# A hybrid decoder block: 576 dense tokens instead of 640, dot products of one gathered tile in the front, and the low parts of v on POOL

## The chip, the cores and the metric

The kernel runs on one core of a Trainium2 chip. The metric is the time of one execution on the device in microseconds; lower is better. The core has a matrix engine (PE), a vector engine (DVE), an activation engine (ACT) and POOL, which also issues the indirect loads; SP issues most other loads and stores. All of them work side by side, each through its own queue, in order.

## The reference

One decoder layer over 1,024 tokens of width 1,024: a mixing part (gated convolution and sliding-window attention) and then a retrieval of experts (PEER). The second part is what the change is about. With `h` the normalised and modulated rows, for each token:

```python
q = (ht @ wq).reshape(t, PEER_HEADS, 2, PEER_DK)          # 8 heads, two halves
sa = einsum('thd,hnd->thn', q[:, :, 0], keys[0]); sb = ...  # 128 scores each
va, ia = top_k(sa, 16); vb, ib = top_k(sb, 16)
cand = va[..., :, None] + vb[..., None, :]                # 256 pairs
top, pos = top_k(cand, 16)
eidx = 128 * ia + ib at pos                               # 16 of 16384 experts for each head
g = softmax(top)
u = u_tab[eidx]; v = v_tab[eidx]                          # 128 rows of 1024 for each token
a = gelu(einsum('thkd,td->thk', u, ht))
out = einsum('thk,thkd->td', g * a, v)
x = x + g2 * out
```

All of it is float32. The kernel computes large products as three products of rounded parts (high times high, high times low, low times high), so each operand is split into a high part (a cast, made by ACT) and a low part (the difference, made by DVE or POOL).

## The kernel before, in words

The expert part is computed in two ways at once. For the *dense* tokens all 16,384 experts are multiplied: the gate weights of a token are spread over a table of 128 x 128 (`spread`, L655), `up` (L779) multiplies all rows of u with the tokens, `weigh1` and `weigh2` apply gelu and the table and split the result, and `down` (L835) multiplies with all rows of v and adds into `dacc`. For the *gathered* tokens, in tiles of 128, `gather` (L691) fetches for each of the 128 chosen experts one row of u for each token (one indirect load of 128 rows, 0.524 MB, issued by POOL at L713), takes its dot product with h on DVE (L732), and then fetches the rows of v and adds them up with their weights on DVE (L740). Before, tokens 0 to 639 are dense and 640 to 1,023 gathered (three tiles).

The front (L307) runs over groups of 384, 384 and 256 tokens: projections (`proj`, L235; 42 for each group, whose low parts POOL makes at L244), attention, the output projection, the rows of x2 and h2 for later, and the scores and choice of keys. While the second and third group pass through the front, the tokens of the group before are chosen and spread: `finish_topk` (L540) with `select` (L565) and `spread`. In a step of `spread` four tokens get their indicator rows `oi` (by ACT, POOL or DVE, as the pattern HOT says, L672 to L679), one DVE instruction makes `oj` (L683) and PE multiplies them.

The dense stage (L750) begins when the front is done. Its loop (L956) goes over j = 4 to 128; a period g is four values of j. In each j `usplit` loads the rows of u for j + 1 and splits them (high on ACT at L771, low on POOL at L772), `up(j)` issues 48 matmuls (L788); in two of four j there is a `down` (L845). The rows of v are loaded and split by `vload` (L820), high on ACT (L831), low on DVE (L832), through a staging tile `vraw` with two buffers: rows 0 to 3 for the first half of the columns before or with phase 0 and 1, rows 0 to 2 for the second half one after another in the first steps of the first `down`, row 3 after it.

What sets the order: `bg(us)` (L202) gives each background task a credit, and a task runs one step for each whole credit; the gather has a rate of 0.49 for each us of credit in the dense stage (L943), the spreading 0.94 in the front. `usplit` gives 2 x 3.2 us, each of the ten steps of `down` in a period 2.57, a projection 24 T / 2400 + 0.5. The dense loop stands in `manual_schedule` (L955), and the trace has POOL's instructions there in the order in which the code is written; in front the order is a planner's. The gather holds a ring of six rows, five in flight.

Of the kernel before, what the change touches and what calls it, by code (L numbers as in the profile page):

```python
# [10 lines left out]
F32 = mybir.dt.float32  # L11
# [10 lines left out]
P = 128  # L22
# [23 lines left out]
DT0, DT = 0, 640  # L46
G0 = 640
GT = 3
J = 4
TB = 32  # L50
HOT = "APVV"
RATE0, RATE = 0.0, 0.49
# [10 lines left out]
TM = 384  # L63
RING = 6
XB = 4
# [9 lines left out]
def hymba_peer_kernel(ctx: ExitStack, tc: tile.TileContext, a, out: bass.AP):  # L75
# [5 lines left out]
    gat = ctx.enter_context(tc.tile_pool(name="gat", bufs=1))  # L81

# [27 lines left out]
    x2d = dram.tile([S, D], F32, name="x2d")  # L110
    h2d = dram.tile([GT * P, D], F32, name="h2d")
# [38 lines left out]
    def ada(parts, ap, ring, sums=None):  # L150
        n = 0
        for i in parts:
            acc = sums if sums is not None and i == parts[0] else ap.tile([P, D], F32, name="acc", bufs=1)
# [9 lines left out]
            if i < 5:  # L163
                mps = pm.tile([P, 8], F32, name="pm")
                for m in range(NC):
                    PE.matmul(mps[:, m:m + 1], acc[:, P * m:P * (m + 1)], ones[:, 0:1], start=True, stop=True)
                V.tensor_add(mod[:, 8 * i:8 * i + 8], mps, cols[:, COLS["b"][0] + 8 * i:COLS["b"][0] + 8 * i + 8])
            else:
                b2 = ap.tile([P, D], F32, name="b2", bufs=1)
# [12 lines left out]
    def bias_table(ap):  # L182
# [6 lines left out]
        rb = ap.tile([32, NH, P], F32, name="rb", tag="acc", bufs=1)  # L189
# [61 lines left out]
    def norm_stats(chunk, T):  # L251
        pt = pj.tile([P, TM], F32, name="pj")
        for c in range(NC):
            sq = tmp("sq")
            A.activation(sq[:, 0:T], chunk(c), AF.Square)
            PE.matmul(pt[:, 0:T], onesd, sq[:, 0:T], start=(c == 0), stop=(c == NC - 1))
        r = tmp("rstd", bufs=2)
# [32 lines left out]
    def group_stats(chunks, T):  # L290
        pt = pj.tile([P, TM], F32, name="pj")
        for i, src in enumerate(chunks):
            sq = tmp("sq")[:, 0:T]
# [13 lines left out]
    def front(t0, T, hs, nxt):  # L307
        nb = T // P
        nd = max(0, min(nb, (DT - t0) // P))
# [68 lines left out]
        halves = gat.tile([P, 2, 4, 2 * P], F32, name="halves", tag="more")  # L378
# [100 lines left out]
        def to_rows(dst, r0, b, srcs, idn):  # L479
            for h in range(2):  # L480
# [10 lines left out]
                nc.sync.dma_start(dst[r0 + P * b:r0 + P * b + P, 512 * h:512 * h + 512], xt)  # L491

        for b in range(nb):
            to_rows(x2d, t0, b, [x2T], ident)
        if ROWS:
            modulate2()
        for b in range(nb):
            if b >= nd:
                to_rows(h2d, t0 - G0, b, [h2H, h2L], identr)
        if nd:  # L500
            for k in range(2):
                for c in range(NC):
                    src = ch(h2[k], c)[:, 0:P * nd].bitcast(F32)
                    at = slice(t0 - DT0, t0 - DT0 + P * nd)
                    nc.sync.dma_start(h2s[k, :, c, at], src)
# [6 lines left out]
        va = [lv.tile([P, 2 * PH, 16], F32, name="va", bufs=5) for b in range(nb)]  # L512
        iu = [lv.tile([P, 2 * PH, 16], U32, name="iu", bufs=5) for b in range(nb)]
        def keys(ms, qs):
            sc = []
            for b in range(nb):
# [3 lines left out]
                s = lv.tile([P, 2, P], F32, name="sc", bufs=4)  # L520
# [19 lines left out]
        def finish_topk():  # L540
            for b in (range(nb) if ORDER else [*range(nd, nb), *range(nd)]):
                r = yield from select(va[b], iu[b])
                if b < nd:
                    yield from spread(t0 // P + b, *r)
                else:
                    place((t0 - G0) // P + b, *r)
                    placed.append(b)
                    if len(placed) == 1:
                        gtask.append(add(gather(), RATE0))
# [15 lines left out]
    def select(va, iu):  # L565
# [63 lines left out]
        for s, src in ((0, aab), (1, stb)):  # L629
            r = ft(f"pick{s}", tag=("a3", "st3")[s])  # L630
            hot1 = sel.tile([P, PH, 16, 16], BF16, name="hot1")
            V.tensor_tensor(hot1, src.rearrange("p (h k) -> p h k", h=PH).unsqueeze(2).to_broadcast([P, PH, 16, 16]),
# [470 lines left out]
```

## Time and profile before

| | us |
|---|---|
| median of 3 runs | 2,877.46 |
| lowest and highest run | 2,875.39 and 2,883.49 |
| span of the profiled execution | 2,871.6 |

The profile is one execution, whose span was 2,871.6 us. An engine's busy time is the time in which it ran at least one instruction; matmuls overlap in a pipeline, so the duration of one is longer than the distance from one to the next. A group of instructions is those of one line, engine and shape; the idle time beside it is that of the engine just before them, with what ended it. The chain of waits goes back from the last instruction to whatever released each step.

### The profile page before, as it was taken

Reading aid. Unit: us, or ns where it says so; the run is one execution under the profiler, and the core shown is the slowest. Engines: PE = TensorE matmul, PEld = TensorE weight load, DVE = VectorE, ACT = ScalarE, POOL = GpSimd, SP = SyncE. Lnnn points to the kernel's source line nnn. Section 1 sums busy time; section 2 is a strip of 40 time slices with the busy share of each in tenths; the row PEclk is TensorE's granted clock in tenths of the full one; section 3 lists DMA queues with packets and bytes.
Section 4 is the critical chain, followed back from the end, with each engine's and each line's share of the span. In section 5 each row is a group of like instructions: output and inputs, shape, how many; then the busy total and the mean of one; then the engine's idle time right before and its main releaser. Section 6 shows DMA issues by size and latency. Waiting matters only on the chain.

```text
span 2871.6 us, 44952 instructions
## 1 busy us (share of the span) xinstructions
PE 2710.1 (94%) x15567; PEld 2441.8 (85%) x15567; DVE 2391.0 (83%) x4853; ACT 1095.5 (38%) x2193; POOL 1727.9 (60%) x1491
## 2 busy tenths in 40 slices
PE   5999989899888889999999999999999999999998
PEld 3888978788687779889999898999999889989997
DVE  5665899878799778888888898888988888888886
ACT  2455467775476633322222232222223222222221
POOL 3534476665676745666666666666666666656661
PEclk7999989999899989999999999999999999999999
DMA  6647423355334576999999999999999999999995
GB/s 224 230 145 232 123 85 129 139 199 181 99 145 138 203 234 202 347 333 348 331 320 346 348 348 333 348 323 334 337 349 323 324 349 333 331 331 342 331 334 185
DMA packets 345032, 763.69 MB, mean 266 GB/s; under 512 B 31418, under 2 KB 130138, under 8 KB 341860
## 3 DMA queue, kind: packets, MB, share of 16 engines
q0 software_dynamic: 112320, 408.99, 39.2%
q1 hardware_dynamic: 231044, 349.21, 36.4%
q8 instruction: 122, 2.00, 0.3%
q10 hardware_dynamic: 1440, 2.62, 0.2%
q14 instruction: 106, 0.87, 0.1%
HBM read 701.45 MB, written 59.24 MB: 265 GB/s over the span
## 4 chain that ended last, share of the span: by engine, by line
PE 44%; DMA 8%; DVE 6%; issue 4%; POOL 2%; ACT 1%; SPq 0%; DVEq 0%; POOLq 0%; ACTq 0%
PE pv L845 23%; PE pa L788 21%; DMA vraw<-in_v 4%; DMA uraw<-in_uT 2%; DVE pq L740 1%; DVE vdL L832 1%; DVE rows L732 1%; DMA wraw<-in_wq 1%; DVE wdL L815 1%; DVE dacc L864 1%; ACT vdH L831 1%; POOL rows L713 1%; DVE more L732 1%; POOL uL L772 0%; DVE gw L807 0%
## 5 line engine op out<-in xcount | busy, mean ns | idle before, releaser
L788 PE MATMUL pa<-h,uH 128*128 128x320 f32 x4096 | 772.0, 310 | 14.5 <-ACT uH L771 6.3
L788 PEld LDWEIGHTS pa<-h,uH 128*128 128x128 f32 x4096 | 648.2, 189 | 22.0 <-ACT uH L771 7.3
L244 POOL TENSOR_TENSOR wL<-wraw,wH 128x512 fp32r<-128x512 f32 x252 | 360.7, 1440 | 263.2 <-ACT wH L243 224.8
L845 PE MATMUL pv<-vdH,wdH 128*128 128x512 f32 x1275 | 500.2, 392 | 14.7 <-DVE dacc L864 14.5
L845 PE MATMUL pv<-vdL,wdH 128*128 128x512 f32 x1275 | 498.1, 391 | 0.1
L845 PE MATMUL pv<-vdH,wdL 128*128 128x512 f32 x1275 | 497.1, 390 | 0.0
L788 PE MATMUL pa<-h,uL 128*128 128x320 f32 x2048 | 468.9, 310 | 2.9 <-POOL uL L772 2.9
L772 POOL TENSOR_TENSOR uL<-uraw,uH 128x512 fp32r<-128x512 f32 x256 | 343.6, 1343 | 149.5 <-ACT uH L771 140.3
L713 POOL DMA_INDIRECT rows<-in_u,eidx x257 | 259.1, 1008 | 164.7 <-DVE aw L732 100.0
L713 POOL DMA_INDIRECT rows<-in_v,eidx x254 | 252.5, 994 | 160.9 <-DVE pq L740 115.6
L788 PEld LDWEIGHTS pa<-h,uL 128*128 128x128 f32 x2048 | 344.0, 189 | 3.8 <-POOL uL L772 3.8
L740 DVE SCALAR_TENSOR_TENSOR pq<-rows,aw,pq 128x1024 f32<-128x1024 f32 x253 | 324.7, 1284 | 5.0 <-DMA rows<-in_v,eidx 2.5
L864 DVE TENSOR_TENSOR dacc<-dacc,pv 128x512 f32<-128x512 f32 x310 | 212.2, 685 | 137.5 <-PE pv L845 136.7
L831 ACT CAST vdH<-vraw 128x512 fp32r<-128x512 f32 x255 | 152.7, 619 | 437.1 <-DMA vraw<-in_v 386.2
L732 DVE CUSTOM_DVE_ANT_0 rows<-rows,pq 128x1024 f32<-128x1024 f32 x257 | 307.8, 1214 | 10.5 <-DMA rows<-in_u,eidx 10.1
L771 ACT CAST uH<-uraw 128x512 fp32r<-128x512 f32 x256 | 158.4, 620 | 384.1 <-DMA uraw<-in_uT 374.1
L845 PEld LDWEIGHTS pv<-vdH,wdH 128*128 128x128 f32 x1275 | 240.0, 188 | 70.9 <-DVE dacc L864 23.1
L845 PEld LDWEIGHTS pv<-vdH,wdL 128*128 128x128 f32 x1275 | 240.0, 188 | 50.6
L845 PEld LDWEIGHTS pv<-vdL,wdH 128*128 128x128 f32 x1275 | 240.1, 188 | 47.6 <-DVE vdL L832 0.5
L678 POOL TENSOR_SCALAR oi<-iota,tr 128x128 f32<-128x128 f32 x160 | 198.5, 1242 | 109.8 <-PE gps L686 89.4
L832 DVE TENSOR_TENSOR vdL<-vraw,vdH 128x512 fp32r<-128x512 f32 x255 | 193.7, 776 | 74.1 <-ACT vdH L831 73.6
L814 ACT CAST wdH<-gw 128x640 fp32r<-128x640 f32 x128 | 93.1, 728 | 402.6 <-DVE gw L807 393.7
(251 smaller groups left out, 5118.7 us busy)
## 6 DMA issues: line engine op xcount, KB each, us to landing
uraw<-in_uT SPq DMA_DIRECT2D x256, 256.0 KB, 6.3
vraw<-in_v SPq DMA_DIRECT2D x255, 256.0 KB, 6.0
gd<-stage SPq DMA_DIRECT2D x20, 2048.0 KB, 7.5
gt<-gd SPq DMA_DIRECT2D x160, 256.0 KB, 10.2
wraw<-in_w_in SPq DMA_DIRECT2D x108, 256.0 KB, 2.8
wraw<-in_wq SPq DMA_DIRECT2D x96, 256.0 KB, 2.8
wt<-in_w_ada SPq DMA_DIRECT2D x40, 512.0 KB, 4.7
wraw<-in_w_out SPq DMA_DIRECT2D x48, 256.0 KB, 2.7
```

What stands on the lines that cost most here:

```text
L244: G.tensor_tensor(wL, w, wH.bitcast(F32), op=ALU.subtract)
L678: (G if who == "P" else V).tensor_scalar(oi, iota, tr[:, 0, t:t + 1], tr[:, 2, t:t + 1], op0=ALU.is_equal, op1=ALU.mult)
L713: G.indirect_dma_start(out=r, out_offset=None, in_=table, in_offset=bass.IndirectOffsetOnAxis(ap=eidx[:, ti, k:k + 1], axis=0))
L732: V.tensor_tensor_reduce(out=r, in0=r, in1=h2, op0=ALU.mult, op1=ALU.add, scale=1.0, scalar=0.0, accum_out=aw[:, k:k + 1])
L740: V.scalar_tensor_tensor(acc, r, aw[:, k:k + 1], acc, op0=ALU.mult, op1=ALU.add)
L771: A.copy(uH, raw)
L772: G.tensor_tensor(uL, raw, uH.bitcast(F32), op=ALU.subtract)
L788: PE.matmul(AT[j][:, s, 0:n], l[:, c, :], h2[r][4 * h + c][:, s * n:s * n + n], start=(h == 0 and c == 0 and k == 0), stop=(h == 1 and c = ...
L831: A.copy(vH, raw)
L832: V.tensor_tensor(vL, raw, vH.bitcast(F32), op=ALU.subtract)
L845: PE.matmul(pt, l[:, P * tt:P * tt + P], r, start=(m == 0), stop=(m == 3 * J - 1))
L864: V.tensor_tensor(dst, dst, pt, op=ALU.add)
```

## The change

- **Tokens.** Dense are tokens 128 to 703 (576), gathered are 0 to 127 and 704 to 1,023 (448), in four tiles of 128, 64, 128 and 128. The tile of 64 puts half of each token's experts on the other 64 partitions, has 64 fetches of u and of v, and its two halves are added by a second, accumulating store.
- **Early dot products.** A ring of four rows (`rowring`) lives through the kernel. From the second group on a task runs the first 129 units of the gather (h and all 128 dot products of tile 0) on three of its rows, with h in the fourth, at a rate of 0.5; what is left of it is drained before the dense stage. In the dense stage the gather goes on with eight rows, seven in flight.
- **Dense products.** `up` runs over two halves of 288 columns, one PSUM bank each (three buffers). `down` takes the rows of v as the stationary operand and 288 tokens as the moving one: 16 outputs of 12 matmuls for a period, where there were 10 of 12 with 512 columns. The sum is kept transposed, and the last step multiplies with g2 and adds x2 in one instruction. A second output holds the dense tokens transposed, and the host only puts rows in place.
- **Low parts of v** are made by POOL instead of DVE.
- **Small.** u is loaded in one DMA for each j (two buffers of that); the pattern of the indicator rows gives DVE three of eight instead of four; the choice of keys works on four heads at a time; some staging buffers are fewer.

The diff, cut to its core:

```diff
-DT0, DT = 0, 640
-G0 = 640
-GT = 3
+DT0, DT = 128, 576
+HN = DT // 2
+GTILES = [(0, 128), (704, 64), (768, 128), (896, 128)]
-HOT = "APVV"
-RATE0, RATE = 0.0, 0.49
+HOT = "APVAVAPV"
+RATEA, RATE = 0.5, 0.5
+GPLAN = []
+for _gi, (_, _w) in enumerate(GTILES):
+    GPLAN += [("h", _gi, 0)] + [("u", _gi, k) for k in range(_w)]
+    GPLAN += [("v", _gi, k) for k in range(_w)] + [("g", _gi, 0), ("x", _gi, 0)]
+NA = 129
-XB = 4
+XB = 3
+    rowring = gat.tile([P, 4, D], F32, name="ring")
...
-        for b in range(nb):
-            to_rows(x2d, t0, b, [x2T], ident)
+        for b, gi in gblocks.items():
+            g0, w = GTILES[gi]
+            to_rows(x2d, GOFF[gi], P - w, b, [x2T], ident)
...
+            for h0 in range(0, PH, 4):
+                hs = slice(h0, h0 + 4)
+                hot1 = sel.tile([P, 4, 16, 16], BF16, name="hot1")
...
+    def gather(plan, slots, held=None):
...
+        ring, at = [], 0
+        for kind, gi, k in plan:
+            while gi not in placed:
                 yield
+            while at < len(plan) and len(ring) < len(slots) - 1 and plan[at][1] in placed:
+                ring.append(fetch(plan[at]))
+                at += 1
             r = ring.pop(0)
+            w = GTILES[gi][1]
+            if kind == "h":
+                h2 = held if held is not None else env["pq"].tile([P, D], F32, name="pq")
+                A.copy(h2, r)
+                aws[gi] = gat.tile([P, P], F32, name="aw", bufs=2)
+            elif kind == "u":
                 V.tensor_tensor_reduce(out=r, in0=r, in1=h2, op0=ALU.mult, op1=ALU.add, scale=1.0,
-                                       scalar=0.0, accum_out=aw[:, k:k + 1])
+                                       scalar=0.0, accum_out=aws[gi][:, k:k + 1])
...
+                if w < P:
+                    A.copy(r[0:w, :], acc[0:w, :])
+                    G.dma_start(at_out, r[0:w, :], accum_op=ALU.add)
...
-                    raw = da.tile([P, 4, P], F32, name="uraw", bufs=2)
-                    nc.sync.dma_start(raw, a["uT"][j, :, 4 * h:4 * h + 4, :])
+                    if h == 0:
+                        both = da.tile([P, NC, P], F32, name="uraw", bufs=2)
+                        nc.sync.dma_start(both, a["uT"][j])
+                    raw = both[:, 4 * h:4 * h + 4, :]
...
             A.copy(vH, raw)
-            V.tensor_tensor(vL, raw, vH.bitcast(F32), op=ALU.subtract)
+            G.tensor_tensor(vL, raw, vH.bitcast(F32), op=ALU.subtract)
...
-            for tt in range(nt):
-                bg(2.57)
-                next(extra, None)
-                pt = pv.tile([P, 512], F32, name="pv")
...
+            for x in range(4):
+                for s in range(2):
+                    bg(1.6)
+                    next(extra, None)
+                    pt = pv.tile([P, 512], F32, name="pv")
+                    m = 0
+                    for j in js:
+                        vH, vL = VV[j, dh]
+                        for l, r in ((vH, W[j][0]), (vH, W[j][1]), (vL, W[j][0])):
+                            PE.matmul(pt[:, 0:n], l[:, P * x:P * x + P], r[:, s * n:s * n + n],
+                                      start=(m == 0), stop=(m == 3 * J - 1))
...
-            if g == P // J - 1:
-                V.tensor_tensor(dst, dst, fin["g2"][dh], op=ALU.mult)
-                V.tensor_tensor(dst, dst, fin["x2"][tt, dh], op=ALU.add)
-                A.dma_start(out[r0:r0 + P, ds], dst)
+            if g == last:
+                V.scalar_tensor_tensor(dst, dst, mod[:, 40 + dc:41 + dc], fin[dc][:, s * n:s * n + n],
+                                       op0=ALU.mult, op1=ALU.add)
+                A.dma_start(outT[:, dc, s * n:s * n + n], dst)
...
-        pv = es.enter_context(tc.tile_pool(name="pv", bufs=2, space=PSUM))
+        pv = es.enter_context(tc.tile_pool(name="pv", bufs=3, space=PSUM))
...
+        if not gtask:
+            gtask.append(add(gather(GPLAN[:NA], [rowring[:, x, :] for x in range(3)], rowring[:, 3, :]), RATEA))
         hs, ft = front(t0, T, hs, nxt)
         drain(prev)
         prev = ft
+    drain(gtask[0])
```

## Rows read from the trace of the kernel before

**Rows 1.** The page's first part: busy time, share of the span, instructions.

```profile
PE 2710.1 (94%) x15567; PEld 2441.8 (85%) x15567; DVE 2391.0 (83%) x4853; ACT 1095.5 (38%) x2193; POOL 1727.9 (60%) x1491
```

**Rows 2.** Stretches: length, busy of engines (instructions), PE clock, DMA share, GB/s.

```profile
345.00:740.00 395.00, 358.81 (x2220) 323.98 (x2220) 336.82 (x1126) 261.64 (x616) 245.63 (x190) 0.97 0.41 143
740.00:1050.00 310.00, 261.70 (x1826) 232.49 (x1824) 254.38 (x904) 195.03 (x459) 211.05 (x161) 0.92 0.44 155
...
903.00:953.00 50.00, 40.89 (x300) 37.44 (x299) 47.76 (x94) 29.76 (x69) 41.86 (x30) 0.97 0.48 168
...
1176.00:2810.00 1634.00, 1623.92 (x9117) 1479.29 (x9118) 1426.94 (x1851) 436.79 (x708) 1049.34 (x974) 1.00 0.96 337
```

**Rows 3.** Chain of waits, one dense period: start, length, engine, tile, line, count.

```profile
1356.36 13.62 PE pv L845 x60
1369.98 21.11 PE pa L788 x144
1391.10 13.62 PE pv L845 x60
1404.72 7.04 PE pa L788 x48
```

**Rows 4.** Groups of POOL, 1,300 to 2,500 us: busy us, mean ns, idle before.

```profile
L772 POOL TENSOR_TENSOR uL<-uraw,uH 128x512 fp32r<-128x512 f32 x172 | 230.6, 1340 | 82.1 <-ACT uH L771 75.2 <-PE pa L788 4.6
L713 POOL DMA_INDIRECT rows<-in_u,eidx x187 | 186.7, 998 | 116.0 <-DVE aw L732 73.6 <-issue 18.4 <-DMA out<-rows 12.7
...
L713 POOL DMA_INDIRECT more<-in_v,eidx x87 | 89.0, 1023 | 44.7 <-DVE pq L740 32.4 <-issue 9.1 <-DMA uraw<-in_uT 0.7
```

**Rows 5.** Timeline of PE in the third front: start us, us, instruction.

```profile
1023.07 0.28 PE L247 MATMUL pj<-h2L,wH 128*128 128x256 f32 x1
...
1025.20 0.28 PE L247 MATMUL pj<-h2L,wH 128*128 128x256 f32 x1
```

**Rows 6.** Timeline of POOL in the dense stage: start us, us, instruction, [idle before].

```profile
1719.52 0.95 POOL L713 DMA_INDIRECT rows<-in_u,eidx  x1
1720.78 0.94 POOL L713 DMA_INDIRECT rows<-in_u,eidx  x1 [0.30 <-DVE gw L807]
1721.74 1.31 POOL L772 TENSOR_TENSOR uL<-uraw,uH 128x512 fp32r<-128x512 f32 x1
1723.20 1.36 POOL L713 DMA_INDIRECT more<-in_u,eidx  x1 [0.16 <-issue]
```

**Rows 7.** DMA issues, 1,300 to 2,500 us: count, KB each, us to landing.

```profile
vraw<-in_v SPq DMA_DIRECT2D x171, 256.0 KB, 6.2
```

**Rows 8.** A group of ACT, 1,300 to 2,500 us, columns as in rows 4.

```profile
L831 ACT CAST vdH<-vraw 128x512 fp32r<-128x512 f32 x170 | 101.5, 619 | 290.1 <-DMA vraw<-in_v 252.8 <-PE pv L845 36.8
```

**Rows 9.** Waits, 1,300 to 2,500 us: who for whom, us, times, longest.

```profile
DVE vdL L832 <- ACT vdH L831: 37.5, 29, 3.2
```

**Rows 10.** Groups of DVE, 1,300 to 2,500 us, columns as in rows 4.

```profile
L732 DVE CUSTOM_DVE_ANT_0 rows<-rows,pq 128x1024 f32<-128x1024 f32 x188 | 225.5, 1214 | 10.3 <-DMA rows<-in_u,eidx 9.9
L740 DVE SCALAR_TENSOR_TENSOR pq<-rows,aw,pq 128x1024 f32<-128x1024 f32 x168 | 215.6, 1284 | 1.7
L864 DVE TENSOR_TENSOR dacc<-dacc,pv 128x512 f32<-128x512 f32 x215 | 147.3, 685 | 98.1 <-PE pv L845 97.7
L832 DVE TENSOR_TENSOR vdL<-vraw,vdH 128x512 fp32r<-128x512 f32 x170 | 128.8, 775 | 37.6 <-ACT vdH L831 37.5
```

**Rows 11.** Groups of DVE, 345 to 1,050 us; last row before that.

```profile
L678 DVE TENSOR_SCALAR oi<-iota,tr 128x128 f32<-128x128 f32 x320 | 129.7, 443 | 24.4 <-PE gps L686 22.4
L683 DVE TENSOR_TENSOR oj<-iota,tr 128x512 f32<-128x512 f32 x160 | 118.9, 764 | 8.2 <-PE gps L686 4.2 <-ACT tr L662 3.2
...
L161 DVE SCALAR_TENSOR_TENSOR acc<-wt,cond,acc 128x1024 f32<-128x1024 f32 x31 | 47.5, 1532 | 6.7 <-DMA wt<-in_w_ada 6.4
```

**Rows 12.** A stretch of 20 us, columns as in rows 2.

```profile
2640.00:2660.00 20.00, 20.00 (x105) 17.64 (x104) 17.32 (x18) 2.56 (x4) 12.24 (x13) 1.00 1.04 390
```

More of the change, by code (lines that the diff above doesn't have):

```diff
@@ L152, in ada @@
         for i in parts:
-            acc = sums if sums is not None and i == parts[0] else ap.tile([P, D], F32, name="acc", bufs=1)
+            acc = sums if sums is not None and i == parts[0] else rowring[:, 0, :]
             for c in range(NC):
@@ L376, in front @@
         mc, ma = bigt(bb, "mc", F32R), bigt(bb, "ma", F32R)
[L378 removed]
+        halves = t1.tile([P, 2, 4, 2 * P], F32, name="halves")
         def attention():
@@ L540, in finish_topk @@
         def finish_topk():
-            for b in (range(nb) if ORDER else [*range(nd, nb), *range(nd)]):
+            for s0, b in blocks:
                 r = yield from select(va[b], iu[b])
[L543 to L549, printed above, removed]
+                lo, hi = max(s0, DT0), min(s0 + P, DT0 + DT)
+                if hi > lo:
+                    yield from spread(s0, lo - s0, hi - s0, *r)
+                if b in gblocks:
+                    place(gblocks[b], *r)
+                    placed.append(gblocks[b])
         return hn, finish_topk()
@@ L688, in spread, with rows_of, fetch @@
                 yield
-            nc.sync.dma_start(gd[(ti * P - DT0) // TB + q], stage)
-    def gather():
+            nc.sync.dma_start(gd[(s0 - DT0) // TB + q], stage)
+    def gather(plan, slots, held=None):
         state = {"n": 0}
-        rows = gat.tile([P, 4, D], F32, name="rows", tag="stage"), gat.tile([P, RING - 4, D], F32, name="more")
         def row():
-            n = state["n"] % RING
+            n = state["n"] % len(slots)
             state["n"] += 1
-            return rows[n // 4][:, n % 4, :]
-        def fetch(u):
-            ti, n = divmod(u, 2 * P + 2)
+            return slots[n]
+        def rows_of(r, src, gi, whole=True):
+            w = GTILES[gi][1]
+            part = src[GOFF[gi]:GOFF[gi] + w, :]
+            G.dma_start(r[P - w:P, :], part)
+            if w < P and whole:
+                G.dma_start(r[0:w, :], part)
+        def fetch(unit):
+            kind, gi, k = unit
@@ L715, in fetch @@
-            return r
-        total = GT * (2 * P + 2)
-        ring = [fetch(u) for u in range(RING - 1)]
-        for u in range(total):
-            while (u + RING - 1) // (2 * P + 2) >= len(placed) and len(placed) < GT:
+            elif kind == "x":
+                rows_of(r, x2d, gi, whole=False)
+            else:
+                G.indirect_dma_start(out=r, out_offset=None, in_=a[kind],
+                                     in_offset=bass.IndirectOffsetOnAxis(ap=eidx[:, gi, k:k + 1], axis=0))
@@ L940, in ahead @@
                 weigh2(j)
-        for t in gtask:
-            t[1], t[2] = RATE, GC0
+        rows = gat.tile([P, 4, D], F32, name="rows", tag="stage")
+        slots = [rows[:, x, :] for x in range(4)] + [rowring[:, x, :] for x in range(4)]
+        add(gather(GPLAN[NA:], slots), RATE, GC0)
         m = 0
```

241 lines of the change are left out of this document (114 added, 127 removed).

## The prediction, made before the run

> **What bounds the kernel now.** I read the busy shares first: PE 94%, DVE 83%, POOL 60% [rows 1]. The windows by stage then show two kernels in one. In the two front stages (345 to 740 and 740 to 1,050 us) DVE is the fullest beside PE, 336.8 of 395 and 254.4 of 310 us, and neither is full. In the dense stage (1,176 to 2,810) PE is busy for 1,623.9 of 1,634 us, beside DMA at a share of 0.96 and 337 GB/s [rows 2]. The chain of waits in the dense stage is PE alone for long stretches: 60 matmuls of L845 in 13.62 us, 144 of L788 in 21.11, 60 in 13.62, 48 in 7.04, together 55.4 us [rows 3]. That is one period, four values of j. The measured period is 55.8 us: L772 makes the low part of u twice for each j, and its 172 instructions stand in 1,200 us, so 13.95 us for each j [rows 4]. So PE is the pace, with 0.4 us lost in each period. The question is what PE costs afterwards, and which engine is next.
>
> **PE.** From the chain a 320-column matmul takes 21.11/144 = 0.1466 us and a 512-column one 0.227 [rows 3]; a 256-column one of the front takes (1025.20 - 1023.07)/18 = 0.118 [rows 5]. Between 256 and 320 columns lie 288, at 0.1325 us. The columns shrink by a tenth, the fixed part of each matmul stays, and the down product issues 192 matmuls of 288 columns in a period where it issued 120 of 512; up has 192 as before. So PE needs 384 x 0.1325 = 50.9 us, 4.5 less than 55.4.
>
> **POOL in the dense stage.** The credits for the gather give (4 x 6.4 + 16 x 1.6) x 0.5 = 25.6 fetches in a period (before: (25.6 + 25.7) x 0.49 = 25.1). POOL makes 8 low parts in a period today, all of u; the 8 of v come to it, so 16. A low part takes 1.34 us in the mean, a fetch 1.00 to 1.02 [rows 4]. The timeline shows what busy time hides: from one fetch to the next 1.26 us pass (1719.52 to 1720.78) though the fetch itself takes 0.95; a low part behind a fetch starts at once, and a fetch behind a low part 0.15 us after it [rows 6]. In the written order the 16 low parts stand in 11 runs, so 11 gaps of 0.15 and 14.6 of 0.30 make 6.0 us. Best case, with the short durations of the timeline: 25.6 x 0.94 + 16 x 1.31 + 6.0 = 51.0 us. With the means: 25.6 x 1.00 + 16 x 1.34 + 6.0 = 53.0. I take the middle, 51.9, as DVE gives up 8 instructions that read the same memory beside it. POOL alone then needs more than PE.
>
> To that comes a wait. The staging tile of v has two buffers. In the second half of a period's v, the third row set can be loaded only when the low part of the first is made. Its load lands 6.2 us after issue [rows 7], and ACT casts it in 0.62 [rows 8]: 6.8 us. Between the two, POOL has one more low part and 1.6 fetches with their gaps, about 3.3 us, as the down steps now come every 12 matmuls of 288 columns. It stands still for the other 3.5. Today the same wait stands on DVE, whose steps are longer: 37.5 us in 21.5 periods, 1.7 each [rows 9]. Behind a standing POOL are queued the next fetches and low parts; DVE is covered by seven rows in flight, PE by the low parts made one j ahead, and both only put off the wait, since POOL never catches up. So the period is 51.9 + 3.5 = 55.4 us. Bounds: 51.3 (no wait; PE's 50.9 with today's loss) and 56.5 (means, the whole wait). Against 55.8 that is -0.4 us in 1,634/55.8 = 29.3 periods: **-12 us**.
>
> **DVE and DMA in the dense stage** are not next. DVE is busy for 87% of 55.8 us, 48.7, today [rows 2]; 8 x 0.775 of v go, and 16 adds of 288 columns at about 0.45 stand for 10 of 0.685 [rows 10] (between 0.385, in proportion, and the 0.685 of the whole; 0.45 as part of it is fixed): 43 of 55.4. A period moves 25.6 fetches of 0.524 MB, 2.1 MB each of u and v, and 18 instead of 20 blocks of the gate table: 18.8 MB, at 55.4 us 339 GB/s, today's rate. Faster, it would become a bound (rival 2).
>
> **Front.** The 128 dot products of tile 0 are new here, as tokens 0 to 127 leave the dense part. Their task starts with the second group and earns 0.5 for each us of credit: 42 projections x 4.34 x 0.5, less what passes until tile 0 is chosen, some 86 units in that group, the rest in the third. The fetches are POOL's, about 1 us each; it is idle for 248 of these 705 us [rows 2]. On DVE a unit costs at least the 1.20 us of busy time that L732 shows with its second operand in PSUM [rows 10]. Here both operands lie in SBUF, and the nearest row with two of 1,024 columns, the accumulation of L161, has 1,532 ns [rows 11] against 1,284 for L740, whose sum is in PSUM [rows 10]. Bounds 1.20 and 1.61 (1.53 and a twentieth for the read of the sum), value 1.40 between them: 179 us. Taken away: half a block of spreading, and an eighth of the indicator rows, which pass from DVE to ACT. Today 160 steps cost 129.7 + 118.9 = 248.6 us [rows 11]; 144 steps of 1.5 x 0.405 + 0.743 = 1.35 us cost 195, so -54. Picking in halves of four heads doubles 12 instructions of a block, in six blocks here, each with a fixed part between nothing and the 0.44 us of a whole small one (L678), 0.15 taken: +11. Together +136 on 591 us of DVE in 705. The fullest stretch of the rows has DVE at 47.8 of 50 us, 95.5% [rows 2]; at that share 727 us need 761: **+56 us**. Bounds: 702 us of work at 100% give -3, 754 at 95.5% +84.
>
> The Trainium skill ("SBUF — State Buffer", section "Who interferes with whom") has a rule against exactly these units: a VectorE instruction with two SBUF inputs and a GpSimd instruction that reads SBUF lock each other out for the whole instruction. The slow L161 agrees with it. By the rule alone the units would go at the upper bound, and the whole would come to 2,940.
>
> **Small terms.** Nine up products before the steady part: 432 x 14.1 ns, -6 us. The last two down products and one closing instruction instead of three: -3. Fewer, larger stores of h2 and four blocks of x2 turned to rows instead of eight lie under the front's DVE; without that cover they give a few us. The second write of the 64-token tile waits on POOL for its first, once, about one landing (6.2). The smaller counts of staging buffers in front get nothing, as no row prices them.
>
> **Sum.** 2,871.6 (span) + 56 - 12 - 6 - 3 = 2,906.6. The median of the three runs, 2,877.46, lies 5.9 us above this span, so I forecast 2,912; its own range is 2,875 to 2,965. A difference below 0.3% (8.6 us) counts as no change.
>
> **Rivals.**
> 1. PE stays the pace (the faster side). Its place is POOL's queue at the third v load: if POOL runs behind and finds its tiles ready, the wait is gone, and with fetches at 0.94 POOL needs 51.0. The point is a POOL period below 51.3 us. Price: -4.5 x 29.3 = -132, with +56 - 9: span 2,786.6, **2,792**. For it: POOL is idle for 36% of the dense stage today, mostly for DVE's rows, and eight row slots instead of six ease that. Against: the 51.0 is a floor without one wait.
> 2. DMA becomes the pace. 337 GB/s at 0.96 is 351 at a full share: 18.8 MB in 53.6 us, -64 + 47: **2,860**. For it: 0.96 over 1,634 us. Against: one stretch of 20 us has 390 GB/s [rows 12], so a full share is no wall.
> The skill ("DMA: Bandwidth & Descriptors", section "Bandwidth") gives some 358 GB/s as a core's part of HBM; that would be 52.5 us and 2,828, but the 390 lies above it.
> 3. The front swallows the dot products: DVE's 114 idle us take them, as PE has a block less to spread in the second group. +5 instead of +56: **2,861**.
> 4. Both prices at their upper ends, period 56.5 and front +84: +21 instead of -12, and +28: **2,973**. Early units that are late (two rows in flight) and drained before the dense part belong here too.
>
> **Chances.** Forecast 0.46, rival 1 0.20, rival 2 0.11, rival 3 0.12, rival 4 0.11. Faster by over 0.3% is rival 1, most of 2, half of 3 and a little of the forecast: 0.37. Within 0.3%: 0.11. Slower: 0.52. The range 2,790 to 2,985 leaves out half of rival 1 and less than half of rival 4.
>
> **What would show it.** Right: POOL busy for 90% or more of the steady part, with little idle time before fetches and a wait for ACT's cast before the low parts of v; PE's matmuls 0.1325 us apart with gaps before L845's successor put down to POOL; a period near 55.4 us; DVE above 90% from 345 us on, and the dense part beginning some 50 us later. If PE runs through at 51 us a period, or the front is no longer than before, the forecast is wrong.

## Result, and the profile after

The kernel became slower: 3,149.03 us against 2,876.7, a ratio of 1.0943 (95% interval 1.0915 to 1.0971). The forecast was 2,912 with a range up to 2,985, so the time lies outside it. The profiled execution after has a span of 3,152.8 us, 281.2 more than before.

The first matmul of the up product ends the front. It starts at 1,045.5 us before and at 1,266.7 after: front +221.2 us, where the forecast had +56. What follows took 1,826.1 us and takes 1,886.1: +60.0, where the forecast had -21. Both terms failed, the front by more.

The page's first part (answers to [rows 1]): PE is busy for about as long as before (2,710.1 us) in a longer span, POOL for 428 us more, DVE for only 44 more.

```profile
PE 2707.2 (86%) x17743; PEld 2548.0 (81%) x17743; DVE 2435.5 (77%) x5083; ACT 1115.6 (35%) x2420; POOL 2155.8 (68%) x1865
```

The windows of the two front stages and of the dense stage, columns as in [rows 2]. DVE is busy for 422.82 of 507 and 321.68 of 402 us, 82%, not the 95.5% that the forecast took; PE's granted clock is 0.83 and 0.85. In the dense stage PE is busy for 1,189 of 1,300 us.

```profile
357.00:864.00 507.00, 383.85 (x1964) 330.18 (x1964) 422.82 (x1244) 244.95 (x580) 328.50 (x257) 0.83 0.60 199
864.00:1266.00 402.00, 309.62 (x1917) 273.38 (x1915) 321.68 (x983) 241.68 (x582) 249.61 (x205) 0.85 0.50 170
1500.00:2800.00 1300.00, 1189.05 (x8628) 1171.86 (x8627) 1010.36 (x1519) 330.47 (x640) 1035.66 (x943) 0.97 0.93 327
```

Groups of the front after (357 to 1,266 us; columns as in [rows 4]). The early products (L759) take 179.1 us, 1,407 ns each: the term of the forecast to the microsecond. Beside them stand the early fetches on POOL, 1,260 ns each instead of "about 1 us", with 121.6 us of standing still before them.

```profile
L759 DVE CUSTOM_DVE_ANT_0 ring<-ring 128x1024 f32<-128x1024 f32 x128 | 179.1, 1407 | 36.4 <-DMA ring<-in_u,eidx 36.4
L707 DVE TENSOR_TENSOR oj<-iota,tr 128x512 f32<-128x512 f32 x144 | 105.0, 733 | 19.0 <-PE gps L710 17.6 <-ACT tr L686 0.6
L702 DVE TENSOR_SCALAR oi<-iota,tr 128x128 f32<-128x128 f32 x216 | 102.0, 475 | 66.3 <-PE gps L710 64.2 <-PE pm L408 1.0 <-PE pj L257 0.4
...
L254 POOL TENSOR_TENSOR wL<-wraw,wH 128x512 fp32r<-128x512 f32 x164 | 231.5, 1421 | 71.2 <-ACT wH L253 59.3 <-PE pj L257 4.5 <-PE pm L533 4.5
L741 POOL DMA_INDIRECT ring<-in_u,eidx x128 | 161.2, 1260 | 121.6 <-DVE aw L759 48.7 <-DVE oi L702 24.9 <-issue 9.9
L702 POOL TENSOR_SCALAR oi<-iota,tr 128x128 f32<-128x128 f32 x144 | 159.1, 1105 | 119.0 <-PE gps L710 104.7 <-ACT oi L699 9.3 <-ACT tr L686 2.3
```

The waits of PE in the same stretch (who for whom: us, times, longest): for POOL's indicator rows, for DVE's, for POOL's low parts of the weights. Each is short, and each holds the projections queued behind it on PE.

```profile
PE gps L710 <- POOL oi L702: 34.2, 36, 3.6
PE gps L710 <- DVE oi L702: 29.8, 25, 4.9
PE pj L257 <- POOL wL L254: 25.7, 32, 2.2
```

POOL's groups in the dense stage after (1,500 to 2,800 us; columns as in [rows 4]):

```profile
L862 POOL TENSOR_TENSOR vdL<-vraw,vdH 128x512 fp32r<-128x512 f32 x183 | 244.0, 1346 | 62.1 <-ACT vdH L861 58.6 <-issue 1.7
L803 POOL TENSOR_TENSOR uL<-uraw,uH 128x512 fp32r<-128x512 f32 x180 | 233.1, 1295 | 2.7 <-ACT uH L802 0.6
L741 POOL DMA_INDIRECT ring<-in_u,eidx x160 | 156.7, 979 | 51.1 <-issue 28.6 <-DVE aw L759 11.0 <-DMA out<-ring 6.2
L741 POOL DMA_INDIRECT rows<-in_u,eidx x160 | 156.7, 979 | 56.8 <-issue 27.5 <-DVE aw L759 20.4 <-DMA out<-rows 2.2
L741 POOL DMA_INDIRECT ring<-in_v,eidx x123 | 121.6, 989 | 39.1 <-issue 23.2 <-DVE pq L768 9.3 <-DVE dacc L895 4.5
L741 POOL DMA_INDIRECT rows<-in_v,eidx x123 | 119.8, 974 | 42.0 <-issue 20.7 <-DVE pq L768 12.5 <-DVE dacc L895 4.9
```

And the waits of the same stretch that matter. PE stands still for a bank of the up product that DVE's gw has to free; POOL for ACT's cast; the two rows of "issue" are the gaps around POOL's own fetches.

```profile
PE pa L817 <- DVE gw L836: 85.1, 38, 8.4
POOL vdL L862 <- ACT vdH L861: 58.6, 36, 3.3
POOL ring L741 <- issue: 51.8, 210, 0.6
POOL rows L741 <- issue: 48.2, 187, 0.6
```

The 180 low parts of u between the 60th and the 240th make 22.5 periods. Their starts give 58.02 us a period after and 56.42 before. These periods make 35.9 of the 60.0 us. Another 25.2 lie between the first matmul of the up product and the 60th low part (421.0 us after, 395.8 before; 385.1 in e2, which has no low parts of v); the rest of the stage is 1.1 us shorter.

### The profile page after: what moved, and what is told of

The parts are those of the page before. It is cut to its first block, busy times and chain, and to the rows that moved or that the text cites. A ratio compares the mean times of both kernels' runs of the same rounds, so it can differ in the third digit from the quotient of the medians.

```text
span 3152.8 us, 49815 instructions
## 1 busy us (share of the span) xinstructions
PE 2707.2 (86%) x17743; PEld 2548.0 (81%) x17743; DVE 2435.5 (77%) x5083; ACT 1115.6 (35%) x2420; POOL 2155.8 (68%) x1865
## 4 chain that ended last, share of the span: by engine, by line
PE 48%; DVE 25%; DMA 9%; issue 9%; POOL 7%; ACT 2%; another core or an unknown queue 0%; SPq 0%; POOLq 0%; DVEq 0%; ACTq 0%
PE pv L876 18%; PE pa L817 16%; PE pj L257 6%; DVE pq L768 4%; DMA ring<-in_u,eidx 3%; DVE ring L759 3%; PE gps L710 3%; DMA vraw<-in_v 2%; DVE rows L759 2%; POOL ring L741 2%; POOL oi L702 2%; DVE dacc L895 1%; POOL vdL L862 1%; POOL wL L254 1%; PE pm L408 1%
## 5 line engine op out<-in xcount | busy, mean ns | idle before, releaser
L817 PE MATMUL pa<-h,uH 128*128 128x288 f32 x4096 | 865.8, 306 | 150.9 <-DVE gw L836 120.4
L876 PE MATMUL pv<-wdH,vdH 128*128 128x288 f32 x2040 | 605.3, 297 | 24.4 <-DVE dacc L895 17.3
L817 PE MATMUL pa<-h,uL 128*128 128x288 f32 x2048 | 623.0, 304 | 3.4 <-POOL uL L803 3.0
L876 PE MATMUL pv<-wdH,vdL 128*128 128x288 f32 x2040 | 602.8, 295 | 1.8 <-POOL vdL L862 1.8
L876 PE MATMUL pv<-wdL,vdH 128*128 128x288 f32 x2040 | 601.5, 295 | 0.7 <-DVE wdL L845 0.7
L741 POOL DMA_INDIRECT ring<-in_u,eidx x288 | 317.9, 1104 | 172.7 <-DVE aw L759 59.7
L862 POOL TENSOR_TENSOR vdL<-vraw,vdH 128x512 fp32r<-128x512 f32 x255 | 340.4, 1347 | 124.2 <-ACT vdH L861 119.6
L876 PEld LDWEIGHTS pv<-wdH,vdH 128*128 128x128 f32 x2040 | 383.5, 188 | 33.0 <-DVE dacc L895 22.1
L876 PEld LDWEIGHTS pv<-wdH,vdL 128*128 128x128 f32 x2040 | 383.4, 188 | 2.5 <-POOL vdL L862 2.5
L876 PEld LDWEIGHTS pv<-wdL,vdH 128*128 128x128 f32 x2040 | 383.3, 188 | 1.0 <-DVE wdL L845 1.0
L768 DVE SCALAR_TENSOR_TENSOR pq<-ring,aw,pq 128x1024 f32<-128x1024 f32 x223 | 285.8, 1281 | 20.1 <-DMA ring<-in_v,eidx 15.1
```

The costliest lines, as they stand in the source:

```text
L741: G.indirect_dma_start(out=r, out_offset=None, in_=a[kind], in_offset=bass.IndirectOffsetOnAxis(ap=eidx[:, gi, k:k + 1], axis=0))
L768: V.scalar_tensor_tensor(acc, r, aw[:, k:k + 1], acc, op0=ALU.mult, op1=ALU.add)
L817: PE.matmul(AT[j, s][:, 0:n], l[:, c, :], h2[r][4 * h + c][:, s * n:s * n + n], start=(h == 0 and c == 0 and k == 0), stop=(h == 1 and c = ...
L862: G.tensor_tensor(vL, raw, vH.bitcast(F32), op=ALU.subtract)
L876: PE.matmul(pt[:, 0:n], l[:, P * x:P * x + P], r[:, s * n:s * n + n], start=(m == 0), stop=(m == 3 * J - 1))
```

## Experiments

Each kernel is the changed one with the edit shown. "Dense from" is the start of the first up matmul in the profiled execution, "period" is taken as above. Kernels with one letter ran on the same chip; ratios are to the kernel before on that chip, with the 95% interval.

| kernel | chip | us | ratio | dense from | period |
|---|---|---|---|---|---|
| e1_vl_dve | A | 3,096.8 | 1.0745 [1.0719, 1.0771] | 1,260.4 | 56.5 |
| e2_no_vl | A | 2,959.0 | 1.0281 [1.0251, 1.0311] | 1,255.4 | 52.0 |
| e3_no_dots | A | 2,956.9 | 1.0257 [1.0220, 1.0293] | 1,118.5 | 56.7 |
| e4_dots_no_fetch | A | 3,004.2 | 1.0421 [1.0394, 1.0448] | 1,176.8 | 56.4 |
| e5_oi6 | B | 3,052.5 | 1.0587 [1.0549, 1.0624] | 1,226.1 | 56.3 |
| e6_vraw3 | B | 3,035.2 | 1.0532 [1.0496, 1.0568] | 1,252.9 | 54.9 |
| e7_banks | B | 3,088.3 | 1.0716 [1.0685, 1.0748] | 1,262.4 | 56.2 |
| e8_half | B | 3,068.0 | 1.0655 [1.0611, 1.0699] | 1,261.8 | 55.4 |
| c0_after | C | 3,159.9 | 1.0953 [1.0919, 1.0986] | 1,262.0 | 58.5 |
| e9_no_link | C | 3,181.4 | 1.1030 [1.0992, 1.1068] | 1,281.1 | 58.5 |
| e10_apart | C | 3,134.3 | 1.0861 [1.0814, 1.0907] | 1,260.3 | 57.9 |
| e11_no_dots_oi6 | C | 2,991.7 | 1.0370 [1.0342, 1.0398] | 1,091.0 | 58.7 |
| c1_after | D | 3,156.6 | 1.0962 [1.0922, 1.1003] | 1,262.3 | 58.4 |
| e12_fetch_sp | D | 3,075.9 | 1.0714 [1.0677, 1.0752] | 1,177.2 | 58.4 |
| e13_all | D | 3,027.8 | 1.0525 [1.0501, 1.0550] | 1,226.3 | 55.7 |
| e14_no_dots_apvv | D | 2,959.1 | 1.0289 [1.0266, 1.0313] | 1,057.3 | 58.7 |
| e15_no_wdl | D | 3,097.8 | 1.0755 [1.0713, 1.0797] | 1,250.2 | 57.1 |
| e16_oi6_apvv | D | 3,112.3 | 1.0784 [1.0746, 1.0822] | 1,213.0 | 58.7 |

**The chip.** The front is much the same on all four (1,250 to 1,267 us wherever it is unchanged). The period isn't: 56.3 to 56.7 on A and B (e3, e4 and e5, which differ from the changed kernel only in front), 58.4 to 58.7 on C and D, with the same dense program; so periods are compared within a letter. The kernel before doesn't show it (medians 2,881.0, 2,876.3, 2,884.9, and 2,875.2 and 2,882.5 on D).

### The front

The early dot products left out (`range(_w if _gi else 0)` for the units of kind "u", `NA = 1`):

> Leaves out the 128 early dot products of tile 0 with their fetches (zeros stand for their sums); all else of the front stays. The dense stage began at 1,267 us after and at 1,066 before. Theory A: all that the front grew by is the early units, fetch and product: the dense stage begins at 1,060 to 1,085 us, and the kernel takes about 2,960 us. Rival D: half or more of it is the rest of the redesign in front (picks in halves, the indicator rows on ACT, fewer staging buffers): it begins at 1,160 us or later, and the kernel takes 3,045 us or more.

The dense stage began 148 us earlier, at 1,118.5, between the two theories' starts and still 73 us later than before. So 148 of the 221 us are the early units, and the other 73, a third, are not.

Products without fetches:

```diff
+            if held is not None and kind == "u":
+                if k < 3:
+                    V.memset(r, 0.0)
```

> Leaves out the 128 early fetches: the dot products run on rows that stay in the ring (zeros), so DVE does all its work and POOL and the DMA queue have none of it. Theory A: most of what the front grew by over the forecast is the wait for rows (two in flight) and POOL's place in order, not DVE's work: the dense stage begins at about 1,130 us, where the forecast's DVE sum put it, and the kernel takes about 3,015 us. Rival E: DVE's work itself is the price: it begins at 1,230 us or later, and the kernel takes 3,115 us or more.

1,176.8, between the two theories' starts: DVE's whole work of the early products costs 58 us (over 1,118.5), the fetches the other 85 to 90. One thing more differs. Without a fetch no product waits for the choice of keys, and the first runs at 270 us instead of 401, so this front has a head start. Theory A here was that the wait for rows is what the fetches cost. The next two kernels ask for that. First both run, but the products need no row (`G.indirect_dma_start(out=slots[k % 2], ...)`, products on `slots[2]`):

> The early fetches and the early dot products both run, but the products read a row that stays (zeros), so DVE doesn't wait for rows and POOL doesn't wait for DVE; leaves out the use of the fetched rows. Without fetches the dense stage began at 1,176.8 us, with both linked at 1,253 to 1,267. Theory A (two rows in flight: the wait for rows is the price): it begins at 1,175 to 1,200 us, 3,010 to 3,050 us in all. Rival J (POOL's time is the price: 128 fetches of 1.25 us stand before the indicator rows and the low parts of the weights that PE waits for): it begins at 1,235 us or later, 3,085 us or more.

1,281.1 against 1,262.0 beside it: no gain at all. DVE waits for no row here, so DVE's wait for rows (36.4 us in the changed kernel) is not the price. The edit did less than meant for POOL, though. The fetches still share two rows, and POOL now stands still until an earlier fetch has landed: 104.3 us (351 to 1,281 us), where c0_after has POOL waiting for 51.7 us for DVE to free a row (354 to 1,262). PE in turn waits longer for POOL's indicator rows, 59.6 us instead of 34.8:

```profile
POOL ring L737 <- DMA ring<-in_u,eidx: 104.3, 61, 5.8
PE gps L710 <- POOL oi L702: 59.6, 48, 5.3
```

So theory A falls for DVE; what two rows in flight cost on POOL is not shown. Then the same amount of bytes through SP (`nc.sync.dma_start(slots[k % 2], a["u"][P * k:P * k + P, :])`):

> As with fetches and products uncoupled (the products read a row of zeros that stays), but the early 128 loads go through SP's queue, 128 rows in their order instead of chosen ones: the same bytes at about the same times, and none of it on POOL; leaves out the choice and the use of the rows. Uncoupled on POOL the dense stage began at 1,281 us, without fetches at 1,177. Theory J (POOL's time is the price): it begins at 1,170 to 1,200 us. Rival L (the bytes are the price: they delay the weight loads that the projections wait for): it begins at 1,240 us or later.

1,177.2, as without fetches. So the bytes, which SP asked for between 229 and 752 us (POOL between 390 and 1,090), cost nothing here, and what is left as the price is the place of the fetches in POOL's queue: 161.2 us of running and 121.6 of standing still before them, which no run separates. The head start is in this kernel too, with the first product at 275 us against 397 in c1_after. It leads c1_after by 40 us at the 33rd product and by 85 at the end of the front, so some 45 us were gained behind that point; the first 40 may in part be the head start. The waits of PE in this front (371 to 1,177 us), to be held against those of the changed kernel above, fall by 7.8, 11.9 and 8.0 us:

```profile
PE gps L710 <- POOL oi L702: 26.4, 35, 2.3
PE gps L710 <- DVE oi L702: 17.9, 18, 4.0
PE pj L257 <- POOL wL L254: 17.7, 21, 2.4
```

And one row of its windows, columns as in [rows 2]:

```profile
371.00:1177.00 806.00, 654.35 (x3870) 567.42 (x3870) 711.35 (x2194) 485.87 (x1162) 443.52 (x334) 0.90 0.53 187
```

DVE is busy for 711 of 806 us here and for 744.5 of 909 in the changed kernel. Up to the dense stage PE's 5,456 matmuls take 966.3 us here, at a granted clock of 0.90 and with 211 us of standing still; in the changed kernel they take 1,000.6 at 0.86 with 266, in c1_after 990.4 at 0.87 with 272. So 24 to 34 of the 85 to 90 us are PE itself, at a lower clock beside more standing still.

Now the 73 us without early units. Six row buffers instead of four, in the whole kernel and without the early units (`name="oi", bufs=6`, `name="aw", bufs=1`):

> Six buffers instead of four for the indicator rows (oi) of the front, and one instead of two for the sums of the dot products to make room. Without the early dot products the front is still 73 us longer than before (dense stage at 1,118.5 us against 1,045.5), while DVE is busy for less of it (558 of 763 us against 585 of 699). Theory F: four buffers are one step of four rows, so ACT, DVE and POOL each wait for the PE matmuls of the step before and PE then waits for them; two more buffers take most of that back: the dense stage begins 45 to 70 us earlier (1,200 to 1,220 us), about 3,090 us in all. Rival G: the rows' new owners (three of eight on ACT, at two instructions a row) set the pace of a step; then it begins less than 15 us earlier, 3,135 us or more.

> Leaves out the early dot products with their fetches (zeros for their sums), and has six buffers for the indicator rows. Without the dot products alone the dense stage began at 1,118.5 us, 73 us later than in the kernel before. Theory F (the four buffers are the rest of the price in front): it begins at 1,060 to 1,080 us, about 2,910 us in all. Rival G (the rows' owners or the narrower halves are): later than 1,100 us, 2,940 us or more.

Six is also what the kernel before had. 36 us earlier than 1,262 in the whole kernel, short of the expected 45 to 70, and 27 (1,118.5 to 1,091.0) without the early units: theory F holds for a part only, and its 1,060 to 1,080 was missed. Then the old share of the rows, `HOT = "APVV"`:

> No early dot products and fetches (zeros for their sums), six row buffers, and the indicator rows in the old share (one on ACT, one on POOL, two on DVE). With the new share the dense stage began at 1,091 us, 46 us later than before. Theory G (three of eight rows on ACT, at two instructions a row, slow each step): it begins at 1,045 to 1,065 us. Rival M (the order of the work in front, above all half a block more of rows in the last group with nothing beside it, is the rest): it begins at 1,080 us or later.

1,057.3: another 34 us (theory G), and 12 us are left over the kernel before, no more than unchanged fronts differ by. Its front has DVE busy for as long as that of the kernel before, in about as long a stretch. Of this kernel:

```profile
358.00:1057.00 699.00, 605.17 (x3878) 543.71 (x3876) 584.01 (x2043) 432.95 (x1016) 426.19 (x334) 0.92 0.40 145
```

and of the kernel before:

```profile
347.00:1045.00 698.00, 615.92 (x4021) 552.53 (x4019) 584.20 (x1982) 453.27 (x1068) 453.74 (x348) 0.95 0.42 147
```

Both repairs in the whole kernel:

> Six buffers for the indicator rows and their old share (one on ACT, one on POOL, two on DVE) in the whole kernel with its early dot products; nothing is left out. Without the dot products these two took 61 us from the front (1,118 to 1,057). If they do so beside them, the dense stage begins at about 1,195 us and the kernel takes about 3,090 us on a chip with a period of 58.5, 3,030 on one with 56.4. If DVE, which has the dot products and more rows again, is full there, it begins at 1,220 us or later.

1,213.0, in between: 49 us earlier than 1,262.3, not 67. With DVE busy for 761 of 856 us (357 to 1,213) the old share of rows gives back 13 us, not 34.

### The dense stage

The low parts of v back on DVE (`V.tensor_tensor(vL, ...)`), and left out (`VV[j, dh] = (vH, vH)`):

> The low parts of v go back to DVE; the rest of the redesign stays. The changed kernel's dense stage takes 58.8 us a period, and PE waits there for banks of the up product that DVE's gw frees. Theory A: the low parts of v on POOL are the loss, because runs of three of POOL's low parts hold back DVE's wdL (1,447 ns in the mean after, 1,034 before) and because POOL waits for ACT's cast. Then wdL falls to about 1,050 ns, PE's wait for gw falls from 4 us a period to under 1, and the period to 52 to 54 us although DVE has 6.2 us more to do: about 2,975 us. Rival B: the loss is the redesign's, three single banks for the up product and sixteen smaller adds on DVE. Then the period stays at 58 us or more, as DVE has more to do: 3,140 us or more.

> Leaves out the low parts of v: no engine makes them, and the product that used them takes the high part in their place, so PE does as many matmuls. Theory A: PE becomes the pace at 50.9 to 51.5 us a period, and about 2,930 us in all. Rival C: DMA is the pace by itself at about 53.6 us: 2,995 us. Rival B (banks and DVE's adds are the loss): PE waits for gw as before, the period is 57 us or more: 3,095 us or more.

On DVE the period is 56.5 us, on POOL on the same chip 56.4 to 56.7: the move itself is worth nothing there, and neither theory's number came. DVE's wdL does fall, to 0.93 us in the mean, and PE still waits for gw for 56.9 of 1,300 us. Without the low parts of v the period is 52.0 us. Windows of that kernel, columns as in [rows 2]:

```profile
1500.00:2800.00 1300.00, 1285.44 (x9622) 1277.56 (x9621) 1093.15 (x1664) 363.68 (x708) 886.42 (x848) 1.00 1.00 365
```

Its only wait of PE in that stretch:

```profile
PE pa L817 <- DVE gw L836: 14.0, 21, 5.6
```

PE is the pace again, with the same banks and the same adds on DVE, and 365 GB/s flow: rivals B and C of these runs fall. Without these low parts the redesign comes within 1.1 us of the 50.9 of the forecast's PE term; they cost some 4.5 us a period on whichever engine they stand.

Four and two banks (`pa` bufs=4, `pv` bufs=2), a third staging buffer (`vraw` bufs=3), and every other low part on DVE (`(G if x % 2 else V)`):

> Four single banks for the up product instead of three, and two for the down product instead of three; the low parts of v stay on POOL. PE waits for a bank that DVE's gw frees for 85 of 1,300 us, 3.7 us a period. Theory B1 (too few banks): that wait falls by half or more, and no other takes its place: the period falls by 2 us or more, 3,085 us or less. Rival A1 (POOL is the pace): PE's wait for gw turns into a wait for POOL's low parts or for DVE's adds, the period stays within 0.7 us: 3,130 to 3,170 us.

> A third staging buffer for v in the dense stage. POOL stood still before its low parts of v for 58.6 of 1,300 us, behind ACT's cast, which waits for the load: 2.6 us in a period of 57.6. Theory A1 (POOL is the pace of the dense stage, as the prediction had it): the wait goes and the period with it, to about 55 us: about 3,075 us. Rival H (PE waits for banks that a late DVE frees, and POOL only follows): the wait goes, the period stays within 0.7 us: 3,130 us or more.

> Every other low part of v goes back to DVE, so POOL has four of them in a period and DVE four. Theory A1 (POOL is the pace): POOL needs 5.4 us less a period and loses half of its waits for the cast, DVE 3.3 more; neither is full, and the period falls to 53 to 54 us: about 3,030 us. Rival I (DVE is the pace as soon as it has any low part of v, as with all eight of them, where the period was 56.5): the period stays above 55.5 us: 3,090 us or more.

Banks: PE's wait for gw is gone and another has its place, at a period of 56.2 against 56.3 (e5, the unchanged dense stage on that chip). The new wait is for banks of the down product, from which the edit took one, so more banks for the one without fewer for the other were not tried. The longest waits of PE in that kernel:

```profile
PE pv L876 <- DVE dacc L895: 69.8, 27, 4.5
PE pv L876 <- POOL vdL L862: 7.1, 3, 3.9
```

Third buffer: POOL's wait falls from 58.6 (59.8 in e5 on that chip) to 22.0 us and the period from 56.3 to 54.9, as theory A1 has it (about 55). Its row:

```profile
POOL vdL L862 <- ACT vdH L861: 22.0, 19, 2.9
```

Halves: 55.4, just below rival I's bound of 55.5 and far from A1's 53 to 54. With less on POOL and more on DVE, POOL waits for DVE to free rows instead (128.6 us in the four groups, worked out from the same waits).

Lock-out. In one period of the changed kernel POOL makes three low parts in a row:

```profile
1733.52 2.54 POOL L862 TENSOR_TENSOR vdL<-vraw,vdH 128x512 fp32r<-128x512 f32 x2
1736.02 1.28 POOL L803 TENSOR_TENSOR uL<-uraw,uH 128x512 fp32r<-128x512 f32 x1
```

and DVE's wdL, begun 0.1 us after the first, ends 0.6 us after the last; gw and PE come behind it:

```profile
1733.62 4.29 DVE L845 TENSOR_TENSOR wdL<-gw,wdH 128x576 fp32r<-128x576 f32 x1
```

The Trainium skill ("SBUF — State Buffer", section "Who interferes with whom") says that such a pair locks each other out, and this trace agrees: 4.29 us, where the 93 wdL of the kernel before took 1.03 in the mean (1,500 to 2,800 us). Whether it sets the pace was asked by moving low parts apart, and by leaving wdL out:

```diff
-                    for x in ((0, 1), (2, 3), (), ())[ph]:
-                        vload(g, 0, x)
+                    if ph < 2:
+                        vload(g, 0, 2 * ph)
...
+                    def mid():
+                        if j - 1 > NW:
+                            weigh1(j - 1)
+                        if ph < 2:
+                            vload(g, 0, 2 * ph + 1)
```

> The second load and low part of v of a step move behind the first low part of u, so POOL's low parts stand in runs of two with fetches between, not in runs of three; all the work stays. Theory K (lock-out: a run of three holds DVE's wdL back up to 4.85 us, DVE frees PE's bank late): wdL falls from 1.36 us to 1.15 or less, PE's wait for gw by half, and the period by 1.5 us or more against the changed kernel in the same call (-45 us or more). Rival A1 (POOL's sum is the pace, the order does not matter): wdL falls, the time changes by less than 15 us.

> Leaves out DVE's low part of the weighted products (wdL, 1.4 to 1.6 us each, four in a period); PE multiplies with the high part in its place, as many matmuls as before. The instruction that POOL locks out the most is gone, and DVE has 6 us less to do in a period. Theory A1 (POOL's sum is the pace): PE's waits move to POOL's low parts, the period stays within 1 us of that of the kernel beside it. Theory K (the late gw is the pace): PE's wait for gw falls from 70 to 85 of 1,300 us to under 25, and the period by 3 us or more, some 90 us in all.

Apart: wdL took 1.46 us where c0_after has 1.63, but the changed kernel's other two profiles have 1.39 and 1.55 (1,500 to 2,800 us), so it did not clearly fall; the period fell by 0.6, the time by 25.5 us: inconclusive, as the edit did less than meant. Without wdL: 57.1 against 58.7 beside it (e16), between the two theories. PE still waits 60.2 of 1,300 us for gw (88.9 beside it), with wdL gone. Of the 1.6 us, about 1.0 can be POOL's own: its fetches take 947 ns instead of about 973 (25 in a period), its low parts of v 1,301 instead of 1,340 (8). That is nearer to A1, POOL's sum as the pace, with a gw that is late because rows come late; this is argued from the sums, not shown.

### Controls and the sum of the repairs

> The changed kernel once more, beside the other three. In its profiled execution the dense stage had a period of 58.0 us, and in four kernels that have the same instructions there and differ only in front (no early dot products, no early fetches, six row buffers) 56.3 to 56.7. If the difference belongs to the program, the period is 58 again and the time about 3,149 us; if it belongs to that chip or that profile, the period is near 56.4 and the time about 3,100 us.

> The changed kernel once more as a measure for the three beside it. Where other kernels with the same dense stage had periods of 56.3 to 56.7 us in two calls and 58.5 to 58.7 in a third, each call ran on a chip of its own. If the period goes with the chip, it is 56.3 or 58.5 here for this kernel and for e12 and e14 alike; if it goes with the program, it is 58 to 58.5 here.

The changed kernel again has 58.5 and 58.4, as its companions on those chips have: the period goes with the chip, or with the time at which it was used.

> Six row buffers, three staging buffers of v, and every other low part of v on DVE, all in one kernel; nothing is left out. If the parts add up: the front 35 us shorter, and the period down by 1.4 (third buffer) and 1 us (halves) or a little less, as both shorten the same wait: about 2,970 us, still slower than before. If PE's wait for DVE's gw is a floor that neither touches, the period stays above 55 us: 3,010 us or more.

Front 36 us shorter than c1, period 2.8 us less: the parts add up. By the numbers written down it is the other branch that came, a period above 55 us and 3,010 us or more, and PE still waits for gw for 65.2 of 1,300 us, so that floor isn't ruled out. But the 2,970 was worked out from chip B's period; on D it is 3,027.8, 128.8 below c1 and 5.25% above the kernel before. Of the versions that leave nothing out none is faster; e6 on its chip has the same ratio within the intervals.

## Why the prediction was wrong, step by step

- **Front, DVE's work: nearly right.** 179.1 us of products forecast and measured, from a value taken between two far bounds, so that it fits to the microsecond is luck; all of DVE's work grew by 744.5 - 584.2 = 160 us (forecast 136: the rows gave back 41.6 instead of 54, the rest is picking and slower small ones).
- **Front, the share: the step that failed.** "At that share 727 us need 761" made DVE the front's bound. It is not: with the fetches on POOL DVE is busy for only 82%. That its extra work costs 58 us without them, near the forecast's 56, is luck: DVE is busy for 709 of 806 us there (370 to 1,176), 88%, not 95.5%. As the waits read, the front goes by PE's order of matmuls, which waits in turn for POOL, DVE and ACT.
- **Front, POOL's fetches: costed at nothing, measured 85 us,** a head start of the products included. The named cover, 248 idle us in that stage, was no cover: POOL's idle time lies between rows and low parts that PE waits for, and every fetch moves these back.
- **Front, smaller buffers and the new share: costed at nothing and at a gain, measured 27 and 34 us** without the early units. Four buffers are just one step's rows; three rows in eight on ACT take two instructions each. With 58, 85 and the last 12 this makes 216 of the 221 us. That sum closes because each step was taken from the one before; in the whole kernel the two gave 36 and 13.
- **"Two rows in flight", named in rival 4:** as DVE's wait for rows not the cause (e9). As POOL's wait for a free row, 50.0 us in the changed front, it stays open: no run gave the early fetches more rows.
- **Dense, PE's term: right.** In the chain of the changed kernel 96 matmuls of L876 take 12.72 us, 0.1325 each:

```profile
1751.82 12.72 PE pv L876 x96
```

- **Dense, POOL as the pace: right in kind, as far as the runs go.** Busy 1,035.7 us in 1,300, 100 of gaps, 58.6 for ACT's cast: at 58.02 us these are 22.4 periods, so 46.2 + 4.5 + 2.6 = 53.3 a period. The forecast had 51.9 + 3.5 = 55.4 (the middle of its 51.0 and 53.0 is 52.0). What it put at nothing are POOL's waits for DVE to free rows, 66.7 us in the waits, 3.0 a period; 78 of these 105 waits, some 20 us, are no longer than the gap before any fetch. The longest:

```profile
POOL rows L741 <- DVE aw L759: 20.7, 31, 3.8
POOL rows L741 <- DVE pq L768: 12.5, 18, 3.5
POOL ring L741 <- DVE aw L759: 11.3, 17, 2.1
POOL ring L741 <- DVE pq L768: 9.3, 14, 3.3
```

  "DVE is covered by seven rows in flight" looks at DVE alone; POOL stands still whenever DVE is late with a row. These waits and 1.7 us of smaller ones make the 58.0.
- **Dense, the kernel before:** its 55.8 was read from 1,200 us; over the 22.5 periods used here it is 56.4.
- **The signs.** PE's 0.1325 us came. POOL is busy for 80% of the dense stage, not 90; PE's gaps there are put down to DVE's gw, not to POOL; DVE is at 82% in front, not above 90; the dense part begins 221 us later, not 50.
- **Rival 2** falls by 365 GB/s at a share of 1.00, with a period of 52.0 us. The Trainium skill ("DMA: Bandwidth & Descriptors", section "Bandwidth") gives about 358 GB/s for each core when both cores of an HBM domain stream; this kernel runs on one core, and 365 over 1,300 us are more.
- **Rival 1** needed a POOL period below 51.3; it was shown only with the low parts of v taken off every engine. **Rival 3** falls: even without fetches the products cost 58 us, not 5. **Rival 4**, 2,973, had the right sign, but not the size: its front price was DVE's, and nothing was left to drain, as the last early product ran at 1,104 us.

## What to carry to other kernels

The idle time of an engine that works in order does not show by its sum what it can hide. Ask which instruction stands behind the new one, and who waits for that; here 128 instructions of about 1.25 us on an engine idle for a third of its time cost up to 85 us. A count of buffers equal to one step's needs can act as a barrier, whatever the profile before shows of it: two more gave 36 us here. When you add up an engine's time, add its waits for slots that another engine has to free, too.

## What the hardware showed that was not expected

The same dense program has a period of 56.3 to 56.7 us on two chips and 58.4 to 58.7 on two others, though the kernel before has the same time on all four within 0.4%. What differs was not found, and as the chips were used at different times, chip and time are not told apart. And the transfers of one kernel (e2) ran at 365 GB/s for 1,300 us at a DMA share of 1.00 once PE was the pace again.
